# Branch results split into high and low parts where they are made, and eight modulation blocks placed behind branch b

## The chip, the cores and the metric

The kernel runs on one core of one Trainium2 chip. The metric is the device time of one execution in microseconds (us). Three executions before the change gave 1832.02, 1841.4 and 1842.75 us; their median, 1841.4, is the time before. One of them, the one that took 1842.75 us, was recorded by the hardware profiler, and all rows of the trace are from it.

## The reference

The kernel computes one layer of a streaming encoder for two request groups that share weights: one prompt of 1024 tokens and one sample of 64 tokens with a cache of 512 keys. All numbers are float32, the model is 1024 wide.

```
mod = silu(c) @ w_ada + b_ada
sh1, sc1, g1, sh2, sc2, g2 = split(mod, 6)

u = rmsnorm(x, norm1_g) * (1 + sc1) + sh1
sq, sk, sv, mqk, mv, mo, mi, mf, ga, gb = split(u @ w_in)
y_a = stick_breaking(sq, k_all, sv)          # 8 heads x 64
h   = mlstm(conv_silu(mqk), mv, mi, mf)      # 4 heads x 128
y_b = sigmoid(mo) * rmsnorm(h) * ml_norm_g

merged = sigmoid(ga) * (y_a @ w_a) + sigmoid(gb) * (y_b @ w_b)
x = x + g1 * (merged @ w_out)
u2 = rmsnorm(x, norm2_g) * (1 + sc2) + sh2
x = x + g2 * ((silu(u2 @ w_ff_gate) * (u2 @ w_ff_up)) @ w_ff_down)
y = rmsnorm(x, final_g)
```

Stick-breaking attention scores a key by a sigmoid and multiplies it by what the later keys have left over; on the chip this is a matmul for the scores, a scan on VectorE, transposes, and a matmul with the values. `y_a` and `y_b` are 512 columns each. `mod` has 6 x 1024 columns for each of the two groups, and they are computed in 48 blocks of 128 columns.

## The kernel before

**Data.** Activations lie transposed: 128 features on the partitions and all 1088 tokens (64 of the sample, then 1024 of the prompt) along the row. Work on tokens goes by three chunks, 0 to 320, 320 to 704 and 704 to 1088. A float32 product that needs its precision is made of three matmuls in the faster type fp32r (`mm3`, lines 75 to 78): both operands are split into a high part (rounded to fp32r) and a low part (the rest), and high x high, high x low and low x high are summed in PSUM. The helpers that split are `hi_act` (line 47, a copy on ScalarE), `hi_pool` and `lo_pool` (lines 53 and 59, GpSimd) and `lo_dve` (line 56, a subtraction on VectorE).

**Weights.** `w_unit` (lines 61 to 69) loads 512 KB of raw weights through the DMA queue of SyncE (SP) into a ring `wr` of three buffers and lets GpSimd (POOL) split it into the rings `wh` and `wl`. The 32 modulation blocks that are not needed at once load their 512 KB of `w_ada` into the same ring `wr` (tiles `wada`), 8 matmuls each in plain float32, a copy, a transpose and a sum (`ada_blocks`, lines 207 to 227).

**Stages.** Up to about 190 us the kernel normalises the input and computes the first modulation blocks. In the mLSTM stage (to about 500 us) the four mLSTM heads run beside the dense units of the input projection; at its end each head writes one 128 x 1088 tile `yb` to the DRAM scratch `yb_d` (lines 792 to 802). In the attention stage (to about 906 us) four pairs of heads run one after another. Pairs 0 to 2 run beside the units of the gates `ga` and `gb` and the modulation blocks 18 to 39, and each writes one tile `ya` to `ya_d` (line 559). Pair 3 runs beside what the change touches: `load_y` brings the seven tiles back as raw tiles `yr`, POOL splits them by chunk into `yh` and `yl` (seven tiles, three chunks, a high and a low part: 42 instructions), the last eight modulation blocks 40 to 47 follow, and then `branch_b`, which multiplies `y_b` by `w_b` in 24 pieces of 12 matmuls. A piece `ps_b` is copied by ScalarE into `tb`, multiplied by a loaded gate `lgb` on POOL and stored to `pb_d`; `lgb` and `tb` share a ring of four buffers, and `ps_b` has two PSUM banks. Pair 3's own `ya` is split on the spot. Branch a (lines 1025 to 1044, to about 961 us) multiplies `y_a` by `w_a` and adds the loaded `pb`: it needs two loads a piece (`lga`, `lpb`) and has six PSUM banks. `w_out` and the feed-forward follow.

**What sets the order.** The program does not write the engines' orders by hand. A call such as `run(attention(3), chain(fill), 27, 0)` advances an attention generator and a list of dense work beside each other; a scheduler with a timing model then places each instruction on its engine, in which the order of emission is the priority. On the chip each engine works its own list strictly in that order, and so does each DMA queue with the loads and stores given to it.

```
run(attention(3), chain(ada_left[24:32] + [branch_b()]), 27, 0)
```

The functions that the diff touches follow.

Of the kernel before, what the change touches and what calls it, by code (L numbers as in the profile page):

```python
# [8 lines left out]
F32 = mybir.dt.float32  # L9
F32R = mybir.dt.float32r  # L10
# [4 lines left out]
P = 128  # L15
# [20 lines left out]
def trunk(ctx, tc, a, o, dbg=None, stop=None):  # L36
# [9 lines left out]
    def hi_act(out, in_):  # L46
        nc.scalar.copy(out, in_)  # L47
# [4 lines left out]
    def hi_pool(out, in_):  # L52
        nc.gpsimd.tensor_scalar(out, in_, 1.0, 0.0, ALU.mult, ALU.add)  # L53

    def lo_dve(out, in_, h):
        nc.vector.tensor_sub(out, in_, h.bitcast(F32))  # L56

    def lo_pool(out, in_, h):
        nc.gpsimd.tensor_sub(out, in_, h.bitcast(F32))  # L59
# [80 lines left out]
    bif = const.tile([P, 8], F32, name="bif")  # L140


    ya_d = dram.tile([3, P, T], F32, name="ya_d")
    yb_d = dram.tile([4, P, T], F32, name="yb_d")
    ga_d = dram.tile([KB, P, T], F32, name="ga_d")
    gb_d = dram.tile([KB, P, T], F32, name="gb_d")
    pb_d = dram.tile([KB, P, T], F32, name="pb_d")
# [28 lines left out]
    def small(shape, name, tag, dtype=F32, bufs=2, pool=None):  # L176
        return (pool or cur["sb"]).tile(shape, dtype, tag=tag, name=name, bufs=bufs)

    def slot(shape, name, tag, bufs=1, dtype=F32):
        n = 1  # L180
        for d in shape[1:]:
            n *= d
        t = cur["sb"].tile([P, SIZES[tag]], dtype, tag=tag, name=name, bufs=bufs)
        v = t[: shape[0], :n]
        if len(shape) == 3:
            v = v.rearrange("p (x y) -> p x y", y=shape[2])
        return v
# [247 lines left out]
    def attention(p):  # L435
# [73 lines left out]
        for i in range(2):  # L509
            qs, kh, kl, vs = hd[i]  # L510
            for m in range(4):
# [34 lines left out]
                u0, u1 = (0, 64) if i == 0 else (64, 0)  # L546
                nc.scalar.copy(tmp[u0 : u0 + 64], po[u1 : u1 + 64, 0:256])
                nc.vector.tensor_add(ya[u0 : u0 + 64, qc], po[u0 : u0 + 64, 0:256], tmp[u0 : u0 + 64])
                if p == 3 and i == 1:
                    qc = slice(0 if m == 0 else NS + 256 * m, NS + 256 * (m + 1))  # L550
                    hi_act(yh[3][:, qc], ya[:, qc])
                    lo_dve(yl[3][:, qc], ya[:, qc], yh[3][:, qc])
                yield
            if i == 0:
                yield from sample()
                if p == 3:
                    y_tiles(3)
        if p < 3:
            nc.sync.dma_start(ya_d[p], ya)

# [152 lines left out]
    def mlstm(h):  # L715
# [73 lines left out]
        rsqrt_cols(cur["sb"], rd, mx, 9, "h")  # L789
        nc.vector.tensor_mul(hm, hm, rd[:, :, None].to_broadcast([P, 9, P]))  # L790
        yield
        yb = slot([P, T], f"yb{h}", "sg", 2)
        for c in range(3):
            ps = bank("t", f"ps_yb{h}_{c}", 3)
            s, e = CHUNKS[c]
            off = 0
            for tt in CTILES[c]:
                L = TILES[tt][1]
                nc.tensor.transpose(ps[:, off : off + L], hm[:L, tt, :], ident[:L, :L])
                off += L  # L800
            nc.vector.scalar_tensor_tensor(yb[:, s:e], ps[:, : e - s], mlg(h), st.og[:, s:e], ALU.mult, ALU.mult)
        nc.sync.dma_start(yb_d[h], yb)
        yield


# [31 lines left out]
    def chain(gens):  # L837
        for g in gens:
            yield from g
# [107 lines left out]
    def y_tiles(b):  # L947
        yh[b] = up.tile([P, T], F32R, tag="u", name=f"yh{b}")
        yl[b] = up.tile([P, T], F32R, tag="u", name=f"yl{b}")

    def load_y(bs):
        raw = {}
        for b in bs:
            raw[b] = up.tile([P, T], F32, tag="u", name=f"yr{b}")
            nc.sync.dma_start(raw[b], ya_d[b] if b < 4 else yb_d[b - 4])
            y_tiles(b)
        for s, e in CHUNKS:
            for b in bs:
                hi_pool(yh[b][:, s:e], raw[b][:, s:e])
                lo_pool(yl[b][:, s:e], raw[b][:, s:e], yh[b][:, s:e])  # L960

    def wide_unit(w, r0, nb, q, name):

# [28 lines left out]
            fill += gs[i : i + 1] + ads[i * na // ng : (i + 1) * na // ng]  # L992
        run(attention(p), chain(fill), 27, 0)
    wb0 = wide_unit(w_b, 0, 4, 0, "wb0")
    load_y(range(4, 8))
    for b in range(3):
        load_y([b])
    run(attention(3), chain(ada_left[24:32] + [branch_b()]), 27, 0)
    ph.close()


# [578 lines left out]
```

## Time and profile before

| | |
|---|---|
| time before, median of 3 (range) | 1841.4 us (1832.02 to 1842.75) |
| profiled execution's own time | 1842.75 us |
| its span in the trace | 1841.1 us |
| mean granted TensorE clock | 0.984 |
| TensorE (PE) busy | 1759.8 us, 96% of the span |
| VectorE (DVE) busy | 1006.8 us, 55% |
| GpSimd (POOL) busy | 677.5 us, 37% |
| ScalarE (ACT) busy | 671.0 us, 36% |

The span runs from the first to the last recorded instruction. Each row of the trace names a line of the kernel, an engine, an operation, the tiles it writes and reads (buffer numbers left out), shapes, a count and, in brackets, how long the engine stood idle before it and what ended the wait. A row of a timeline begins with the start time and the duration. A row for one tile (`yh<-yr x21: 448/512/2427`) gives the count, then shortest, median and longest duration in ns, then first and last start. `SPq` marks what SP issues to its DMA queue. The granted clock is the share of full speed that TensorE was allowed.

### The profile page before, as it was taken

The page shows a single profiled execution, that of the slowest core. Times are in us where ns is not written, and L with a number is a line of the kernel's source. Part 1 is how long each engine was busy: PE and PEld are TensorE (multiplying, and loading weights), DVE is VectorE, ACT ScalarE, POOL GpSimd, SP SyncE. Part 2 cuts the span into 40 slices and gives each one's busy share as a digit, 9 for nine tenths or more (in the row PEclk, how much of TensorE's full clock was granted, in tenths as well). Part 3 has the DMA queues.
Part 4 walks back from the last instruction along what each step waited for, and adds up shares of the span by engine and source line. Part 5 has one row for each costly group of instructions (what it writes and reads, how often), then busy time and mean ns, then how long its engine had stood idle before and what let it go on. Part 6 is the DMA issues. An engine that isn't in the chain of part 4 may idle for free. (4 is left out here: it accounts for less than half of the span.)

```text
span 1841.1 us, 31721 instructions
## 1 busy us (share of the span) xinstructions
PE 1759.8 (96%) x12388; PEld 1693.1 (92%) x12388; DVE 1006.8 (55%) x1903; ACT 671.0 (36%) x1401; POOL 677.5 (37%) x554
## 2 busy tenths in 40 slices
PE   5899999999999999988989999999999999999997
PEld 4699999999889888967979999999999999999997
DVE  6633424252267667785463488754555775544435
ACT  5332424343244444444313555532233543101006
POOL 2434645453433132387566330122222002354324
PEclk9999999999999999989999999999999999999999
DMA  9426667654756465694566246632222676443102
GB/s 268 112 81 198 164 189 154 196 126 137 173 149 145 122 150 134 157 264 133 174 192 186 72 140 196 180 92 79 71 77 77 207 203 197 159 144 114 47 12 98
DMA packets 313208, 265.54 MB, mean 144 GB/s; under 512 B 13670, under 2 KB 285282, under 8 KB 313058
## 3 DMA queue, kind: packets, MB, share of 16 engines
q1 hardware_dynamic: 301026, 224.67, 41.4%
q0 software_dynamic: 12032, 38.84, 9.2%
q8 instruction: 98, 1.61, 0.4%
q14 instruction: 52, 0.43, 0.1%
HBM read 206.62 MB, written 77.84 MB: 155 GB/s over the span
## 5 line engine op out<-in xcount | busy, mean ns | idle before, releaser
L76 PE MATMUL ps_fd<-hh,wh_fd 128*128 128x384 f32 (+1 forms) x480 | 157.1, 327 | 1.2 <-DVE hst L1348 1.2
L78 PE MATMUL ps_fd<-hh,wl_fd 128*128 128x384 f32 (+1 forms) x480 | 157.2, 327 | 0.0
L77 PE MATMUL ps_fd<-hl,wh_fd 128*128 128x384 f32 (+1 forms) x480 | 157.1, 327 | 0.0
L56 DVE TENSOR_TENSOR w<-wr,w 128x512 fp32r<-128x512 f32 x140 | 95.6, 694 | 38.5 <-ACT w L47 35.5
L1432 DVE SCALAR_TENSOR_TENSOR x1f<-ps_fd,mod,x1f 128x384 f32<-128x384 f32 (+2 forms) x128 | 60.4, 497 | 101.3 <-PE ps_fd L78 101.3
L390 DVE TENSOR_TENSOR_SCAN re<-re 128x128 f32<-128x128 f32 (+3 forms) x64 | 105.5, 1651 | 15.7 <-ACT re L386 15.4
L47 ACT CAST w<-wr 128x512 fp32r<-128x512 f32 x140 | 85.2, 620 | 74.7 <-PE ps_gc L1356 21.1
L53 POOL TENSOR_SCALAR wh_fd<-wr_fd 128x1024 fp32r<-128x1024 f32 x20 | 24.6, 1232 | 227.1 <-PE ps_ga L1356 119.4
L76 PEld LDWEIGHTS ps_fd<-hh,wh_fd 128*128 128x128 f32 x480 | 90.1, 188 | 1.4 <-POOL wl_fd L59 1.4
L78 PEld LDWEIGHTS ps_fd<-hh,wl_fd 128*128 128x128 f32 x480 | 90.1, 188 | 0.0
L77 PEld LDWEIGHTS ps_fd<-hl,wh_fd 128*128 128x128 f32 x480 | 90.1, 188 | 0.0
L47 ACT CAST hh<-hr 128x1088 fp32r<-128x1088 f32 (+1 forms) x26 | 24.1, 962 | 175.5 <-PE ps_fd L77 151.4
L386 ACT ACTIVATE re<-z 128x512 f32<-128x512 f32 (+2 forms) x96 | 47.3, 494 | 81.5 <-DVE z L382 67.5
L1356 PE MATMUL ps_ga<-b1h,w 128*128 128x272 f32 x352 | 74.3, 290 | 2.5 <-ACT g L1341 1.8
L1356 PE MATMUL ps_gb<-b6h,w 128*128 128x272 f32 x352 | 75.2, 292 | 0.0
L1356 PE MATMUL ps_gd<-b7h,w 128*128 128x272 f32 x352 | 75.0, 292 | 0.0
L1356 PE MATMUL ps_ga<-b2h,w 128*128 128x272 f32 x352 | 74.1, 289 | 0.0
L1356 PE MATMUL ps_gc<-b5h,w 128*128 128x272 f32 x352 | 74.1, 290 | 0.0
L1356 PE MATMUL ps_gc<-b3h,w 128*128 128x272 f32 x352 | 73.7, 288 | 0.0
L1356 PE MATMUL ps_gd<-b4h,w 128*128 128x272 f32 x352 | 73.6, 289 | 0.0
L56 DVE TENSOR_TENSOR al<-ps_a,ah 128x512 fp32r<-128x512 f32 (+1 forms) x80 | 49.4, 630 | 34.2 <-ACT ah L47 33.8
L76 PE MATMUL ps_ga<-uh,wh_ga 128*128 128x384 f32 (+1 forms) x192 | 64.9, 338 | 1.5 <-DVE re L388 1.2
(551 smaller groups left out, 6067.4 us busy)
## 6 DMA issues: line engine op xcount, KB each, us to landing
wada<-in_w_ada SPq DMA_DIRECT2D x48, 512.0 KB
wr<-wsum_d SPq DMA_DIRECT2D x80, 256.0 KB
h_d<-hst SPq DMA_DIRECT2D x44, 272.0 KB
wr<-in_w_ff_gate SPq DMA_DIRECT2D x40, 256.0 KB
wr_fd<-in_w_ff_down SPq DMA_DIRECT2D x20, 512.0 KB
hr<-h_d SPq DMA_DIRECT2D x18, 544.0 KB
wsum_d<-in_w_ff_up POOLq DMA_DIRECT2D x6, 1282.0 KB, 7.8
wsum_d<-in_w_ff_gate POOLq DMA_DIRECT2D x6, 1282.0 KB, 7.8
```

The costliest lines, as they stand in the source:

```text
L47: nc.scalar.copy(out, in_)
L53: nc.gpsimd.tensor_scalar(out, in_, 1.0, 0.0, ALU.mult, ALU.add)
L56: nc.vector.tensor_sub(out, in_, h.bitcast(F32))
L76: nc.tensor.matmul(ps, wh, xh, start=first, stop=False)
L77: nc.tensor.matmul(ps, wh, xl, start=False, stop=False)
L78: nc.tensor.matmul(ps, wl, xh, start=False, stop=last)
L386: nc.scalar.activation(rest[:, c0 : c0 + w], ps, AF.Sigmoid, scale=-scale)
L390: nc.vector.tensor_tensor_scan(r, r, r, 1.0, ALU.mult, ALU.bypass)
L1356: nc.tensor.matmul(ps, w[:, a, j, :], b[j // 2][:, j % 2, :], start=p in (1, 6, 5, 7) and j == 0 and k == 0, stop=j == 3 and k == 2, skip_ ...
L1432: nc.vector.scalar_tensor_tensor(x1[m][:, lo:hi], ps[:, lo - s : hi - s], mod[:, 40 + m, g : g + 1], x1[m][:, lo:hi], ALU.mult, ALU.add)
```

## The change

The two scratch arrays get a second plane, so that each branch result is kept as its high and its low part.

- An mLSTM head (`yb`) no longer collects one tile: for each chunk it makes the piece, splits it with ScalarE and VectorE, and stores both parts. 4 heads x 3 chunks give 12 casts, 12 subtractions and 24 stores, in place of 4 stores.
- An attention pair 0 to 2 splits `ya` in four pieces as they are finished (the first of 320 tokens, with the sample), through two small tiles with one buffer each, and stores both parts: again 12 casts, 12 subtractions and 24 stores, in place of 3.
- `load_y` loads the parts straight into `yh` and `yl`: 14 loads of 544 KB in place of 7, and the 42 instructions on POOL and the raw tiles are gone.
- Beside pair 3, branch b is emitted first and the modulation blocks 40 to 47 behind it.

What is computed and every matmul on it stay the same.

```diff
--- before.py
+++ after.py
@@ -140,8 +140,8 @@
     bif = const.tile([P, 8], F32, name="bif")
 
 
-    ya_d = dram.tile([3, P, T], F32, name="ya_d")
-    yb_d = dram.tile([4, P, T], F32, name="yb_d")
+    ya_d = dram.tile([3, 2, P, T], F32, name="ya_d")
+    yb_d = dram.tile([4, 2, P, T], F32, name="yb_d")
     ga_d = dram.tile([KB, P, T], F32, name="ga_d")
     gb_d = dram.tile([KB, P, T], F32, name="gb_d")
     pb_d = dram.tile([KB, P, T], F32, name="pb_d")
@@ -546,17 +546,22 @@
                 u0, u1 = (0, 64) if i == 0 else (64, 0)
                 nc.scalar.copy(tmp[u0 : u0 + 64], po[u1 : u1 + 64, 0:256])
                 nc.vector.tensor_add(ya[u0 : u0 + 64, qc], po[u0 : u0 + 64, 0:256], tmp[u0 : u0 + 64])
-                if p == 3 and i == 1:
+                if i == 1:
                     qc = slice(0 if m == 0 else NS + 256 * m, NS + 256 * (m + 1))
-                    hi_act(yh[3][:, qc], ya[:, qc])
-                    lo_dve(yl[3][:, qc], ya[:, qc], yh[3][:, qc])
+                    if p == 3:
+                        h_, l_ = yh[3][:, qc], yl[3][:, qc]
+                    else:
+                        h_, l_ = (small([P, 320], f"yp{x}{p}_{m}", f"yp{x}", F32R, bufs=1)[:, : qc.stop - qc.start] for x in "hl")
+                    hi_act(h_, ya[:, qc])
+                    lo_dve(l_, ya[:, qc], h_)
+                    if p < 3:
+                        nc.sync.dma_start(ya_d[p, 0, :, qc], h_.bitcast(F32))
+                        nc.sync.dma_start(ya_d[p, 1, :, qc], l_.bitcast(F32))
                 yield
             if i == 0:
                 yield from sample()
                 if p == 3:
                     y_tiles(3)
-        if p < 3:
-            nc.sync.dma_start(ya_d[p], ya)
 
 
 
@@ -789,7 +794,6 @@
         rsqrt_cols(cur["sb"], rd, mx, 9, "h")
         nc.vector.tensor_mul(hm, hm, rd[:, :, None].to_broadcast([P, 9, P]))
         yield
-        yb = slot([P, T], f"yb{h}", "sg", 2)
         for c in range(3):
             ps = bank("t", f"ps_yb{h}_{c}", 3)
             s, e = CHUNKS[c]
@@ -798,8 +802,15 @@
                 L = TILES[tt][1]
                 nc.tensor.transpose(ps[:, off : off + L], hm[:L, tt, :], ident[:L, :L])
                 off += L
-            nc.vector.scalar_tensor_tensor(yb[:, s:e], ps[:, : e - s], mlg(h), st.og[:, s:e], ALU.mult, ALU.mult)
-        nc.sync.dma_start(yb_d[h], yb)
+            n = e - s
+            yb = small([P, 384], f"yb{h}_{c}", "gt")[:, :n]
+            h_ = small([P, 384], f"ybh{h}_{c}", "sh", F32R)[:, :n]
+            l_ = small([P, 384], f"ybl{h}_{c}", "sl", F32R)[:, :n]
+            nc.vector.scalar_tensor_tensor(yb, ps[:, :n], mlg(h), st.og[:, s:e], ALU.mult, ALU.mult)
+            hi_act(h_, yb)
+            lo_dve(l_, yb, h_)
+            nc.sync.dma_start(yb_d[h, 0, :, s:e], h_.bitcast(F32))
+            nc.sync.dma_start(yb_d[h, 1, :, s:e], l_.bitcast(F32))
         yield
 
 
@@ -948,16 +959,11 @@
         yh[b] = up.tile([P, T], F32R, tag="u", name=f"yh{b}")
         yl[b] = up.tile([P, T], F32R, tag="u", name=f"yl{b}")
 
-    def load_y(bs):
-        raw = {}
-        for b in bs:
-            raw[b] = up.tile([P, T], F32, tag="u", name=f"yr{b}")
-            nc.sync.dma_start(raw[b], ya_d[b] if b < 4 else yb_d[b - 4])
-            y_tiles(b)
-        for s, e in CHUNKS:
-            for b in bs:
-                hi_pool(yh[b][:, s:e], raw[b][:, s:e])
-                lo_pool(yl[b][:, s:e], raw[b][:, s:e], yh[b][:, s:e])
+    def load_y(b):
+        y_tiles(b)
+        src = ya_d[b] if b < 4 else yb_d[b - 4]
+        for t, x in ((yh[b], 0), (yl[b], 1)):
+            nc.sync.dma_start(t.bitcast(F32), src[x])
 
     def wide_unit(w, r0, nb, q, name):
 
@@ -992,10 +998,9 @@
             fill += gs[i : i + 1] + ads[i * na // ng : (i + 1) * na // ng]
         run(attention(p), chain(fill), 27, 0)
     wb0 = wide_unit(w_b, 0, 4, 0, "wb0")
-    load_y(range(4, 8))
-    for b in range(3):
-        load_y([b])
-    run(attention(3), chain(ada_left[24:32] + [branch_b()]), 27, 0)
+    for b in (4, 5, 6, 7, 0, 1, 2):
+        load_y(b)
+    run(attention(3), chain([branch_b()] + ada_left[24:32]), 27, 0)
     ph.close()
 
 
```

The scheduler's order moves with it. First, PE where branch b begins. In the rows `po2_1_3` is the output of attention pair 2, `z3` are scores of pair 3, `ps_ada40` is modulation block 40, `ps_b0_0` the first piece of branch b with the parts `yh4` to `yh7` of `y_b` and the weights `wh_wb0`, `wl_wb0`. Before:

```order
L541 MATMUL po2_1_3_7724<-ah_2_1_3_4_7756,vs2_1_7188 128x256
L217 MATMUL ps_ada40_8967<-wada40_8968,cT_85 32x128 x8
L520 MATMUL z3_0_4_0_8471<-kh3_0_8353,qs3_0_8352 128x512
L521 MATMUL z3_0_4_0_8471<-kl3_0_8354,qs3_0_8352 128x512
L541 MATMUL po2_1_3_7724<-al_2_1_3_4_7757,vs2_1_7188 128x256
L541 MATMUL po2_1_3_7724<-ah_2_1_3_4_7756,vs2_1_7188 128x256
L541 MATMUL po2_1_3_7724<-al_2_1_3_4_7757,vs2_1_7188 128x256
```

After:

```order
L541 MATMUL po2_1_3_7864<-ah_2_1_3_4_7896,vs2_1_7310 128x256
L76 MATMUL ps_b0_0_9070<-yh4_8427,wh_wb0_8423 128x320
L77 MATMUL ps_b0_0_9070<-yl4_8428,wh_wb0_8423 128x320
L78 MATMUL ps_b0_0_9070<-yh4_8427,wl_wb0_8424 128x320
L76 MATMUL ps_b0_0_9070<-yh5_8431,wh_wb0_8423 128x320
L77 MATMUL ps_b0_0_9070<-yl5_8432,wh_wb0_8423 128x320
L78 MATMUL ps_b0_0_9070<-yh5_8431,wl_wb0_8424 128x320
L76 MATMUL ps_b0_0_9070<-yh6_8435,wh_wb0_8423 128x320
L541 MATMUL po2_1_3_7864<-al_2_1_3_4_7897,vs2_1_7310 128x256
L541 MATMUL po2_1_3_7864<-ah_2_1_3_4_7896,vs2_1_7310 128x256
L541 MATMUL po2_1_3_7864<-al_2_1_3_4_7897,vs2_1_7310 128x256
```

Where block 40 stood between two matmuls of pair 2's last output, the first seven matmuls of branch b stand, and its next ones are spread among attention's from there.

Second, PE at the end of branch b; `ps_b7_2` is its last piece and `ps_a0_0` the first of branch a. Before:

```order
L77 MATMUL ps_b7_2_9550<-yl7_8297,wh_wb6_9451 128x384
L78 MATMUL ps_b7_2_9550<-yh7_8296,wl_wb6_9452 128x384
L76 MATMUL ps_a0_0_9625<-yh0_8324,wh_wa0_9617 128x320
L77 MATMUL ps_a0_0_9625<-yl0_8325,wh_wa0_9617 128x320
L78 MATMUL ps_a0_0_9625<-yh0_8324,wl_wa0_9618 128x320
```

After:

```order
L78 MATMUL ps_b7_2_9525<-yh7_8439,wl_wb6_9427 128x384
L217 MATMUL ps_ada40_9544<-wada40_9545,cT_85 32x128 x8
L541 MATMUL po3_1_3_9013<-ah_3_1_3_4_9045,vs3_1_8469 128x256
L217 MATMUL ps_ada41_9560<-wada41_9561,cT_85 32x128 x5
L541 MATMUL po3_1_3_9013<-al_3_1_3_4_9046,vs3_1_8469 128x256
L541 MATMUL po3_1_3_9013<-ah_3_1_3_4_9045,vs3_1_8469 128x256
```

and some rows on:

```order
L217 MATMUL ps_ada46_9640<-wada46_9641,cT_85 32x128 x8
L222 MATMUL ps_ada46_9640<-ident_66,ada_sb46_9651 128x128
L217 MATMUL ps_ada47_9656<-wada47_9657,cT_85 32x128 x8
L222 MATMUL ps_ada47_9656<-ident_66,ada_sb47_9667 128x128
L76 MATMUL ps_a0_0_9728<-yh0_8443,wh_wa0_9720 128x320
L77 MATMUL ps_a0_0_9728<-yl0_8444,wh_wa0_9720 128x320
```

The eight blocks and the last matmuls of attention now stand between the two branches.

Third, SP's queue at the same place. `pb_d<-tb7_1` and `tb7_2` are the stores of branch b's last pieces, `wada` the raw weights of a modulation block, `wr_wa` those of branch a, `lga` and `lpb` the loads for branch a's first pieces. Before:

```order
L983 DMA pb_d_98<-tb7_1_9546 128x384
L983 DMA pb_d_98<-tb7_2_9565 128x384
L1033 DMA lga0_0_9621<-ga_d_96 128x320
L1033 DMA lpb0_0_9623<-pb_d_98 128x320
L1033 DMA lga0_1_9642<-ga_d_96 128x384
L1033 DMA lpb0_1_9644<-pb_d_98 128x384
```

After:

```order
L989 DMA pb_d_98<-tb7_1_9521 128x384
L214 DMA wada43_9593<-in_w_ada 128x8x128
L989 DMA pb_d_98<-tb7_2_9540 128x384
L214 DMA wada44_9609<-in_w_ada 128x8x128
L214 DMA wada45_9625<-in_w_ada 128x8x128
L214 DMA wada46_9641<-in_w_ada 128x8x128
L214 DMA wada47_9657<-in_w_ada 128x8x128
L64 DMA wr_wa0_9718<-in_w_a 128x4x256
L64 DMA wr_wa2_9854<-in_w_a 128x4x256
L64 DMA wr_wa4_9990<-in_w_a 128x4x256
L1038 DMA lga0_0_9724<-ga_d_96 128x320
```

The loads of blocks 43 to 47 and of branch a's first three weights, which stood far ahead of these stores, now stand around and behind them, and ahead of branch a's first gate loads.

## The prediction

> **What bounds the kernel now.** The page comes first.
>
> ```profile
> span 1841.1 us, 31721 instructions
> PE 1759.8 (96%) x12388; PEld 1693.1 (92%) x12388; DVE 1006.8 (55%) x1903; ACT 671.0 (36%) x1401; POOL 677.5 (37%) x554
> ```
>
> TensorE (PE) is busy for 1759.8 of 1841.1 us, so a change gains only by taking away PE idle time (81 us in all), slow clock or PE work. The table by stage shows where these lie; its columns are the stretch, its length, the busy time of PE, PEld, DVE, ACT and POOL with instruction counts, the granted PE clock, the DMA share and GB/s.
>
> ```profile
> 190.00:500.00 310.00, 305.87 (x1968) 298.66 (x1967) 109.59 (x225) 112.24 (x241) 145.07 (x129) 1.00 0.63 161
> 500.00:787.00 287.00, 274.00 (x1920) 249.52 (x1920) 201.52 (x378) 126.55 (x296) 87.59 (x88) 0.98 0.60 146
> 787.00:826.00 39.00, 32.04 (x289) 23.39 (x291) 36.01 (x79) 18.94 (x43) 34.33 (x32) 0.87 0.92 270
> 826.00:839.00 13.00, 11.22 (x86) 10.84 (x78) 5.16 (x14) 5.21 (x13) 13.00 (x15) 1.00 0.33 116
> 839.00:852.00 13.00, 8.94 (x31) 7.47 (x32) 6.02 (x11) 3.60 (x9) 7.77 (x9) 0.74 0.40 127
> 852.00:906.00 54.00, 50.86 (x326) 48.51 (x325) 32.03 (x46) 24.34 (x58) 34.74 (x24) 1.00 0.49 152
> 906.00:961.00 55.00, 49.52 (x293) 47.67 (x291) 30.63 (x43) 10.69 (x27) 35.52 (x29) 1.00 0.66 195
> ```
>
> The stretch that the change rewrites is 787 to 906, between the last gate unit and branch a. In its first 39 us VectorE (DVE) is busy for 36.0 and POOL for 34.3, while PE idles for 7.0 and runs at 0.87 of its clock: attention's scans set the pace and PE has nothing dense beside them. PE's order in time shows why.
>
> ```profile
> 799.08 0.39 PE L541 MATMUL po<-al,vs 128*128 128x256 f32 x1 [1.69 <-DVE al L56]
> 815.12 0.33 PE L222 MATMUL ps_ada<-ident,ada_sb 128*128 128x128 f32 x1 [2.47 <-DVE ada_sb L220]
> 826.26 0.41 PE L76 MATMUL ps_b<-yh,wh_wb 128*128 128x320 f32 x1
> 840.49 0.50 PE L474 MATMUL z0s<-ckl,zq 128*128 128x512 f32 x1 [3.26 <-POOL ckl L53]
> 906.29 0.33 PE L78 MATMUL ps_b<-yh,wl_wb 128*128 128x384 f32 x1
> 906.47 0.31 PE L76 MATMUL ps_a<-yh,wh_wa 128*128 128x320 f32 x1
> ```
>
> Branch b, the dense work of this stretch, begins at 826.3 and ends at 906.6; branch a follows without a gap. What held branch b back is seen in the instructions on the raw tiles `yr`.
>
> ```profile
> L53 POOL TENSOR_SCALAR yh<-yr x21: 448/512/2427, 791.6 to 835.1; 128x384 fp32r<-128x384 f32 x14, 128x320 fp32r<-128x320 f32 x7
> L59 POOL TENSOR_TENSOR yl<-yr,yh x21: 857/1000/2498, 793.1 to 841.5; 128x384 fp32r<-128x384 f32 x14, 128x320 fp32r<-128x320 f32 x7
> L955 SPq DMA_DIRECT2D yr<-yb_d x4: 338/392/479, 782.5 to 785.6; - x4
>   DMA yr<-yb_d: 7.6, 1
> ```
>
> Loads go out from 782.5, POOL waits until 791.6 and then splits 42 pieces until past 841.
>
> **The change, part by part.** Times are the profiled execution's: span 1841.1, its own time 1842.75, 1.3 over the median 1841.4 and the highest of the three runs.
>
> POOL issues the loads of an attention head beside those of `yr`.
>
> ```profile
> 780.83 1.12 POOL L430 DMA_DIRECT2D kh<-qk_d  x2 [2.81 <-PE z L521]
> 781.92 0.54 POOL L429 DMA_DIRECT2D qs<-qk_d  x1
> 782.42 0.55 POOL L431 DMA_DIRECT2D kl<-qk_d  x1
> 782.92 0.57 POOL L429 DMA_DIRECT2D qs<-qk_d  x1
> 783.42 0.58 POOL L431 DMA_DIRECT2D kl<-qk_d  x1
> ```
>
> *The split leaves POOL.* All 42 POOL operations go. Two prices rise from it. Eight tiles of 544 KB instead of four must land before branch b's first chunk can end: 4.46 MB at the 270 GB/s of 787 to 826 are 16.5 us, so from 782.5 the last lands near 799. That head's six loads of 64 rows (272 KB each) share the wires: 1.67 MB or 6 us more, so 805 is the late end. I take 803. And the freed POOL no longer slows VectorE:
>
> ```profile
> 755.31 0.42 DVE L391 TENSOR_TENSOR be<-be,re 128x256 f32<-128x256 f32 x1
> 794.75 0.91 DVE L391 TENSOR_TENSOR be<-be,re 128x256 f32<-128x256 f32 x1
> ```
>
> The same product takes 0.42 us beside a quiet POOL and 0.91 beside the splits. A few such pairs make 2 to 4 us of VectorE time in a stretch that VectorE bounds.
>
> *Eight modulation blocks leave the front.* One block is 16 matmul records and a transpose (the row groups two blocks):
>
> ```profile
> 810.15 1.08 PE L217 MATMUL ps_ada<-wada,cT 128*32 128x128 f32 x32 [0.17 <-DVE mod L227]
> ```
>
> Half of 1.08 us and about 0.2 for the transpose make 0.75 each, 6 us for eight.
>
> *What this gives up to the end of branch b.* The ceiling: idle time 7.0 + 1.8 + 4.1 + 3.1 = 16.0 (table), clock 32.04 x 0.13 + 8.94 x 0.26 = 6.5, blocks 6: 28.5 us. What comes back: until 803 PE has attention alone, as before (16 us at the 18% idle of that stretch are 3 us), and it is in-order, with branch b's first matmuls standing ahead of attention's, so a tile that lands late stops both: 4 more (0 to 9). The 87 us after it keep the 6% idle of 852 to 906, 5 us, plus 2 for `ckl`, whose 3.26 us wait was for a POOL that is now free. Clock 1.5. So 28.5 - 15.5 = **13 us earlier**, between 5 and 20: branch b ends near 893.
>
> *What the blocks cost behind branch b.* Blocks 43 to 47 need buffers of the three-deep `wr` ring that blocks 40 to 45 hold, and the weights of branch a come behind them in the same ring and on the same SP queue. So once branch b ends there is a chain of loads with nothing dense on PE. How long a 512 KB load takes from issue to its waiting reader is seen twice:
>
> ```profile
> 578.27 0.38 SPq L64 DMA_DIRECT2D wr_gb<-in_w_in  x1
> 582.53 1.04 POOL L53 TENSOR_SCALAR wh_gb<-wr_gb 128x1024 fp32r<-128x1024 f32 x1 [11.36 <-DMA wr_gb<-in_w_in]
> 651.87 0.38 SPq L64 DMA_DIRECT2D wr_gb<-in_w_in  x1
> 661.67 1.04 POOL L53 TENSOR_SCALAR wh_gb<-wr_gb 128x1024 fp32r<-128x1024 f32 x1 [8.87 <-DMA wr_gb<-in_w_in]
> ```
>
> 4.3 us at best, 9.8 at worst. And the end of branch b on POOL, with the splits of branch a's weights:
>
> ```profile
> 907.11 1.01 POOL L982 TENSOR_TENSOR tb<-tb,lgb 128x384 f32<-128x384 f32 x1 [2.37 <-DMA lgb<-gb_d]
> 909.56 1.01 POOL L982 TENSOR_TENSOR tb<-tb,lgb 128x384 f32<-128x384 f32 x1 [0.42 <-DMA lgb<-gb_d]
> 910.53 2.40 POOL L59 TENSOR_TENSOR wl_wa<-wr_wa,wh_wa 128x1024 fp32r<-128x1024 f32 x1
> 914.39 0.87 POOL L1039 TENSOR_TENSOR lga<-lga,lpb 128x320 f32<-128x320 f32 x1 [1.46 <-DMA lpb<-pb_d]
> ```
>
> The last two products end 1.5 and 4.0 us after the last matmul of branch b (906.6), and SP's order puts the load of block 43 behind the store of the one, 44 and 45 behind the other. From branch b's end: load 43 goes out at 2.0, 44 and 45 at 4.5 and 4.9. They land at 6.3, 8.8 and 10.7 (512 KB at 270 GB/s is 1.9 us, so the third waits for the wire). Block 45 computes by 11.3, its buffer takes the first weights of branch a, which land at 15.6; POOL's high part (1.04) opens branch a at 16.7, with 12 matmuls that need no low part (2 us), and the low part is there 2.4 us later, at 19. PE meanwhile has 6 us of blocks. Branch a starts in effect **17 us after branch b's end**, where it was 0: 14 if the loads overlap better, 26 at 9.8 us a load.
>
> The Trainium skill ("DMA: Bandwidth & Descriptors", section "Anatomy of one DMA — SWDGE (gpsimd) path") fits a DMA as 2.0 us plus bytes over 436 GB/s, 3.2 us for 512 KB. By it the two loads in series would be 2 us shorter and the gap an estimated 15 us. The 4.3 us of the row is the time here, so it stands.
>
> *After a gap PE's clock is low:* 839 to 852 ran at 0.74, 13 x 0.26 = 3.4 us lost. I take 2.5 (0 to 4). *Branch a's own queue:* POOL holds three splits (3.4 us each) ahead of the first `lga` sum, which so comes some 10 us after branch a's start instead of 8: 2 us (0 to 4), hidden by six PSUM banks at first.
>
> *Where the splits went.* 24 casts on ScalarE (ACT) and 24 subtractions on VectorE:
>
> ```profile
> L47 ACT CAST yh<-ya 128x256 fp32r<-128x256 f32 (+1 forms) x4 | 1.7, 428 | 2.0 <-DVE ya L548 2.0
> L56 DVE TENSOR_TENSOR yl<-ya,yh 128x256 fp32r<-128x256 f32 (+1 forms) x4 | 3.0, 744 | 0.5 <-ACT yh L47 0.5
> ```
>
> 10 us on the one, 18 on the other. Before 500, half of each lies under PE at 305.87 of 310; without that cover it would be 14 us. The `sh` ring is now shared with the q and k results, so a cast waits for a store two back: 0 to 1 us for each head. In 500 to 787 VectorE is busy for 201 of 287, and 6 us more there delay attention a little. SP also gets 41 more stores, of which some wait ahead of weight loads with a ring's slack. Together +2 (-2 to 6).
>
> **The sum:** -13 + 17 + 2.5 + 2 + 2 = +10.5 on 1842.75, or 1853; two of the terms (clock, `lga`) may overlap with each other, so I take **1851**. The parts' ends give 1834 to 1868.
>
> **The rivals.** Bounds first: about 1% (18 us: under 1823, over 1860) is what a measurement tells from no change.
>
> 1. *Slow chain, slower.* The place is the loads between block 43 and branch a's first weights. Near 9 us a load and above, the gap is 26 us and the time 1860. For it: 651.87 to 661.67, and eight 512 KB loads with branch a's first `lga` and `lpb` share that stretch. Against: the quick row, and no attention loads are left by then. 20%.
> 2. *Branch b is no earlier.* It waits for twice the bytes, or SP, held by the store of pair 2's last low part (it stands ahead of `lgb1_0`), starves the four `gt` buffers. Then only the 6 us of blocks are gained: 1858, with a third of its chance above 1860. 13%.
> 3. *The gap is filled.* Attention's tail runs late and covers the chain, or VectorE's relief brings the full 20 us: 1830 to 1840. 11%.
> 4. *No gap at all and the full gain:* 1842.75 - 20 is 1823 and below. Against it stands the ring: a block's buffer frees only after PE has read it. 6%.
>
> The forecast itself has 50%. Slower by over 1%: 26% (rival 1, part of 2, 2% of the forecast); faster by over 1%: 7%; within: 67%. The range that holds 8 in 10 is **1834 to 1867**.
>
> **What will show it.** Right: no `yr` on POOL; the first `ps_b` near 796 to 804 and the last near 893; `ps_ada` in a row behind it with PE mostly idle for 12 to 20 us; POOL's first `wh_wa` ended by a DMA, and `ps_a` from about 910. Wrong: a first `ps_b` after 815 (rival 2), a gap under 8 us (rivals 3, 4) or above 24 (rival 1), or PE idle time before 787 that grew by more than 5 us.

## The result, and the profile after

The changed kernel takes 1860.7 us in the median of five executions against 1841.6 in the median of six before, measured beside it: a ratio of 1.0106 (95% interval 1.009 to 1.0123), about 19 us slower. A sixth execution (4505.21 us), and one of the run ya_split_only below (7697.19 us), fell in a slow state of the chip and are left out. The profiled execution took 1856.07 us, 13.3 more than the profiled one of before. The rows below account for these 13.3; the rest is scatter between executions, since the profiled one of before was the slowest of its series and that of after one of the fastest of its own.

The table by stage starts at 190 us in both kernels and is then cut at the same events: from 190 us to the last transpose of the mLSTM result (`ps_yb`), to the last gate unit (`ps_gb`), to the last matmul of branch b, (after the change) to the first of branch a, to the first of `w_out`, to the end. Columns are the stretch, its length, busy time of PE, PEld, DVE, ACT and POOL, granted PE clock, DMA share, GB/s. Before:

```profile
190.00:482.80 292.80, 292.34 (x1888) 286.10 (x1887) 107.51 (x218) 110.48 (x238) 135.91 (x115) 1.00 0.60 158
482.80:787.50 304.70, 288.02 (x2003) 262.36 (x2001) 203.98 (x386) 128.31 (x300) 96.75 (x102) 0.98 0.63 151
787.50:906.60 119.10, 103.16 (x722) 90.53 (x722) 78.86 (x147) 52.42 (x122) 89.84 (x77) 0.93 0.60 184
906.60:961.70 55.10, 49.62 (x296) 47.70 (x294) 31.33 (x45) 10.43 (x26) 35.79 (x30) 1.00 0.67 195
961.70:1841.10 879.40, 861.34 (x6297) 856.81 (x6294) 494.50 (x906) 297.98 (x573) 247.16 (x167) 0.99 0.41 124
```

After:

```profile
190.00:497.00 307.00, 294.44 (x1875) 287.79 (x1873) 123.43 (x224) 108.96 (x240) 135.29 (x114) 0.98 0.58 153
497.00:802.20 305.20, 282.16 (x2003) 261.32 (x2001) 205.80 (x398) 135.43 (x316) 96.24 (x100) 0.97 0.62 158
802.20:904.60 102.40, 91.27 (x577) 83.38 (x576) 71.44 (x122) 51.38 (x121) 43.24 (x35) 0.93 0.68 211
904.60:921.60 17.00, 11.35 (x145) 6.57 (x144) 7.32 (x29) 1.79 (x5) 2.06 (x2) 0.70 0.89 252
921.60:974.90 53.30, 50.89 (x294) 49.61 (x295) 30.06 (x43) 9.49 (x24) 38.55 (x29) 0.97 0.70 211
974.90:1854.30 879.40, 860.73 (x6294) 855.98 (x6294) 493.54 (x906) 298.62 (x574) 247.57 (x168) 0.99 0.41 124
```

By stage, after minus before: mLSTM +14.2, attention beside the gates +0.5, branch b -16.7, gap +17.0, branch a -1.8, the rest 0.0: together +13.2. Branch b's gain and the gap cancel; what is left is the mLSTM stage, where PE had idled 0.46 us and now idles 12.56 (the other 2.1 us are busy time, at a clock of 0.98 for 1.00). The waits of PE (what waits for what, us in total, times, longest) show on whom. Before the change the largest wait of `ps_yb` was 0.5 us; after it, between 190 and 560:

```profile
PE ps_ga L76 <- ACT gt_ga L823: 15.1, 1, 15.1
PE ps_yb L803 <- DVE hn L795: 11.8, 3, 4.8
```

The second row is the loss of the mLSTM stage: PE stands at the transposes of three heads because VectorE's normalised result `hn` is late. (The first row lies at the start of attention. That stage as a whole is only 0.5 us longer, but ya_split_only below, without the split of `yb`, is 6.1 us shorter there.) Why `hn` is late is seen in the first head. Before, VectorE:

```profile
208.42 1.79 DVE L735 TENSOR_SCALAR wg<-W 128x8 f32<-128x8 f32 x1 [1.32 <-ACT W L733]
212.63 0.22 DVE L84 RECIPROCAL rd<-rs_h 128x9 f32<-128x9 f32 x1 [0.87 <-ACT rs_h L83]
212.88 1.18 DVE L85 TENSOR_TENSOR rs_h<-rd 128x9 f32<-128x9 f32 x1
214.71 1.36 DVE L790 TENSOR_TENSOR hn<-hn,rd 128x1152 f32<-128x1152 f32 x1
```

After, VectorE, then ScalarE, then POOL:

```profile
207.04 4.33 DVE L740 TENSOR_SCALAR wg<-W 128x8 f32<-128x8 f32 x1 [1.32 <-ACT W L738]
215.33 0.22 DVE L84 RECIPROCAL rd<-rs_h 128x9 f32<-128x9 f32 x1 [2.50 <-ACT rs_h L83]
215.58 3.86 DVE L85 TENSOR_TENSOR rs_h<-rd 128x9 f32<-128x9 f32 x1
220.10 1.36 DVE L795 TENSOR_TENSOR hn<-hn,rd 128x1152 f32<-128x1152 f32 x1
...
212.66 1.12 ACT L704 ACTIVATE cs<-cv 128x1091 f32<-128x1091 f32 x1 [3.47 <-DVE mx L792]
213.80 1.28 ACT L83 ACT_TABLE_LOAD   x1
215.09 0.21 ACT L83 ACTIVATE rs_h<-mx 128x9 f32<-128x9 f32 x1
...
207.42 2.91 POOL L705 TENSOR_TENSOR cv<-cv,cs 128x1091 f32<-128x1091 f32 x1
209.95 1.39 POOL L53 TENSOR_SCALAR wh_v<-wr_v 128x1024 fp32r<-128x1024 f32 x1
214.19 2.93 POOL L705 TENSOR_TENSOR cv<-cv,cs 128x1091 f32<-128x1091 f32 x1
216.70 2.71 POOL L59 TENSOR_TENSOR wl_v<-wr_v,wh_v 128x1024 fp32r<-128x1024 f32 x1
```

The work between is the convolution of the next head: `cs` on ScalarE and the product `cv` on POOL. Before, it came behind the normalisation (the two products began at 221.28 and 225.05); now it runs through its middle. ScalarE does `cs` ahead of `rs_h` (VectorE's wait is 2.50 for 0.87): the square root `rs_h` stands behind 1.12 us of `cs` and behind the row ACT_TABLE_LOAD of 1.28 us, which before the change began at 211.09, while `mx` was still being made. And two VectorE operations on 8 or 9 elements a row last 4.33 and 3.86 us, for 1.79 and 1.18, beside POOL's products. The reason is in one removed line of the diff: `yb` had held a slot of the ring `sg`, which has two, and `cs` needs one. With `yb` in small tiles the slot is free, and the scheduler moves the next head's convolution ahead (raw_gt below tests this). The third user of `sg` is `hsq`, the squares of the normalisation itself. The wait of 3.47 us in the first row of ScalarE ends with the sum over them (`mx`, L792), which fits a second `cs` that now takes the slot of `hsq`.

The gap behind branch b, SP's loads first, then PE and POOL:

```profile
905.32 0.38 SPq L214 DMA_DIRECT2D wada<-in_w_ada  x1
915.70 4.35 SPq L64 DMA_DIRECT2D wr_wa<-in_w_a  x3
...
912.64 1.08 PE L217 MATMUL ps_ada<-wada,cT 128*32 128x128 f32 x16 [1.48 <-DMA wada<-in_w_ada]
914.57 1.08 PE L217 MATMUL ps_ada<-wada,cT 128*32 128x128 f32 x16
921.63 0.64 PE L76 MATMUL ps_a<-yh,wh_wa 128*128 128x320 f32 x1 [1.12 <-POOL wh_wa L53]
...
920.53 1.05 POOL L53 TENSOR_SCALAR wh_wa<-wr_wa 128x1024 fp32r<-128x1024 f32 x1 [13.82 <-PE ps_ada L222]
```

The matmul at 912.64 is block 44. Its load went out at 907.36, the first of four in one more row of SP:

```profile
907.36 6.77 SPq L214 DMA_DIRECT2D wada<-in_w_ada  x4
```

So the gap is a chain: 2.7 us until block 41 has freed a buffer, 5.3 for the load of block 44, 3.1 for blocks 44 and 45 (45 begins 1.9 us after 44, behind its copy and transpose; the gap's clock is 0.70), whose second frees the buffer at 915.70, 4.8 for branch a's first weights, 1.1 for their split: 17.0.

### The profile page after: what moved, and what is told of

The parts are those of the page before. It is cut to its first block, busy times and chain, and to the rows that moved or that the text cites. A ratio compares the mean times of both kernels' runs of the same rounds, so it can differ in the third digit from the quotient of the medians.

```text
span 1854.3 us, 31842 instructions
## 1 busy us (share of the span) xinstructions
PE 1758.3 (95%) x12388; PEld 1695.5 (91%) x12388; DVE 1024.3 (55%) x1927; ACT 677.3 (37%) x1423; POOL 634.6 (34%) x512
## 5 line engine op out<-in xcount | busy, mean ns | idle before, releaser
L390 DVE TENSOR_TENSOR_SCAN re<-re 128x128 f32<-128x128 f32 (+3 forms) x64 | 94.5, 1478 | 13.9 <-ACT re L386 13.3
L76 PE MATMUL ps_ga<-uh,wh_ga 128*128 128x384 f32 (+1 forms) x192 | 65.0, 338 | 15.1 <-ACT gt_ga L823 15.1
```

What stands on the lines that cost most here:

```text
L76: nc.tensor.matmul(ps, wh, xh, start=first, stop=False)
L390: nc.vector.tensor_tensor_scan(r, r, r, 1.0, ALU.mult, ALU.bypass)
```

## The experiments

Each run stands beside executions of the kernel before on the same chip. The third column is the time from the first to the last `ps_yb`, which lies in the mLSTM stage alone, as in these rows of the tile before and after the change (218.5 to 482.8 is 264.3). What the first head loses ahead of its `ps_yb` is not in it: that row began at 214.2 to 218.5 us in the runs in which `yb` has its slot, and at 220.2 to 224.1 in those in which it has none. In the table, the fourth column is the gap from branch b's last matmul to branch a's first.

```profile
L799 PE MATMUL ps_yb<-ident,hn x36: 271/273/332, 218.5 to 482.8; 128*128 128x128 f32 x32, 64*128 64x64 f32 x4
```

```profile
L803 PE MATMUL ps_yb<-ident,hn x36: 271/327/473, 221.5 to 497.0; 128*128 128x128 f32 x32, 64*128 64x64 f32 x4
```

| run | ratio to before (95%) | mLSTM heads, us | gap, us |
|---|---|---|---|
| before | 1 | 264.3 | 0.2 |
| the change | 1.0106 (1.009 to 1.0123) | 275.5 | 17.0 |
| order_only | 1.0061 (1.0042 to 1.0081) | 264.3 | 16.7 |
| split_only | 1.0049 (1.0031 to 1.0067) | 277.0 | 0.2 |
| ya_alone | 0.9955 (0.9941 to 0.997) | 264.3 | 0.2 |
| yb_alone | 1.012 (1.0102 to 1.0138) | 275.5 | 3.6 |
| ya_split_only (ya and order) | 0.9991 (0.9974 to 1.0007) | 264.3 | 17.5 |
| yb_in_slot | 1.0046 (1.0028 to 1.0065) | 278.7 | 18.7 |
| slot_mix | 1.0002 (0.999 to 1.0013) | 279.3 | 0.2 |
| inplace_mix | 1.0032 (1.0017 to 1.0047) | 280.4 | 0.2 |
| dead_casts | 0.9987 (0.9975 to 0.9999) | 264.3 | 16.4 |
| raw_gt | 1.0144 (1.0115 to 1.0172) | 277.5 | 16.3 |
| gt3 | 1.0113 (1.0087 to 1.0139) | 275.7 | 18.9 |
| ya_mix | 0.9962 (0.9945 to 0.9979) | 264.2 | 0.2 |
| ya_pieces | 0.9972 (0.9958 to 0.9986) | 264.3 | 0.2 |
| tail3 | 0.9928 (0.9906 to 0.9951) | 264.2 | 6.4 |

**The order alone** (order_only), on the kernel before:

```diff
-    run(attention(3), chain(ada_left[24:32] + [branch_b()]), 27, 0)
+    run(attention(3), chain([branch_b()] + ada_left[24:32]), 27, 0)
```

> The kernel before with only the emission order changed: branch b ahead of blocks 40 to 47, splits on GpSimd as before. Theory 1 (the chain is the order's own cost): a gap of 13 to 20 us between the last matmul of branch b and the first of branch a; the mLSTM stage is unchanged (last ps_yb near 483); branch b gains at most the 6 us of the blocks, so 1848 to 1858, slower than before by 6 to 16. Rival (without the early end the tail of attention covers the loads): 1838 to 1845 and no gap over 8 us.

1.0061 (1852.0 us), as theory 1 had it. The gap is there in full, on an untouched mLSTM stage, so it belongs to the order:

```profile
786.10:898.00 111.90, 94.14 (x577) 85.85 (x576) 76.21 (x121) 51.03 (x119) 73.15 (x74) 0.92 0.52 155
898.00:914.70 16.70, 10.93 (x145) 6.05 (x144) 6.33 (x27) 1.84 (x5) 2.06 (x2) 0.78 0.92 261
```

Branch b's stretch falls by 7.2 us (119.1 before). Its first matmul stands at 800.4 instead of 826.3 although POOL still splits 42 pieces: the blocks ahead of it had held its start, not the splits alone.

**The splits alone** (split_only): the changed kernel with that line as before.

> The changed kernel with blocks 40 to 47 emitted ahead of branch b again. Theory 1 (load chain behind branch b costs 17 us, the blocks in front cost 6 and delay branch b some): branch a follows branch b without a gap over 3 us, the time is 1846 to 1853, 6 to 14 below the changed kernel; the mLSTM stage stays as slow as in the changed kernel. Rival (VectorE's scans or the twice as large loads bound the stretch, and the gap only took up slack that branch b's early end had made): the time stays at 1855 to 1863.

1.0049, the forecast of theory 1: no gap, and the mLSTM stage as slow as in the change.

**`ya` without `yb`** (ya_split_only): the changed kernel with `yb` of before, as one tile in its slot, stored raw and split by POOL at branch b.

> The changed kernel with yb as before (one tile a head, stored raw, loaded raw and split on GpSimd), so that only ya is split where it is made; branch b still ahead of blocks 40 to 47. Theory 1 (the mLSTM stage's loss comes only from the split of yb: slot, rings and stores): from 190 us to the last ps_yb 293 us as before (307 in the changed kernel), gap ahead of branch a 17 us. For the attention stage two outcomes: if the split of ya shortens it (it freed the ya tile earlier), the last ps_gb falls 292 to 299 us behind the last ps_yb (304.8 before) and the time is 1840 to 1846; if not, 303 to 307 and 1847 to 1856, like the kernel with the order alone. Theory 2 (mLSTM stage slow for another reason): last ps_yb at 492 or later.

The ratio is 0.9991 (1836.5 us), better than expected for either outcome, with 299.1 us from the last `ps_yb` to the last `ps_gb`, at the edge of the first. The heads take 264.3 us as before, and the new order with `ya` split costs nothing in sum. So the split of `yb` is worth 1.0106 - 0.9991 = 1.15%, 21 us, all of the change's loss. Between the two profiles it makes the mLSTM stage 14.6 us longer and the stretch from there to the last gate unit 6.1 (305.2 against 299.1), and branch b 5.1 shorter. With `ya` raw and the order alone that stretch was 305.8, so beside the new order the split of `ya` gains there about what the split of `yb` loses. This does not add up as simply in the old order: in yb_alone below, with `ya` raw, it is 298.1.

**Each split alone** (ya_alone, yb_alone), in the order of before.

> The kernel before with the split of ya alone (parts stored per piece, loaded straight into yh and yl); yb raw and split on GpSimd, blocks 40 to 47 ahead of branch b as before. If the parts add up (ya split beside the new order: 0.9991 against 1.0061, so -0.70%), the ratio to before is 0.991 to 0.995, 1822 to 1830 us. Rival (the split of ya only helps the early branch b of the new order): 0.998 to 1.002, 1835 to 1842.

> The kernel before with the split of yb alone (as in the change: no slot, parts in the rings gt, sh and sl); ya raw, order as before. If the parts add up (the change 1.0106 against 0.9991 without the split of yb, so +1.15%), the ratio is 1.010 to 1.014, with the last ps_yb near 497. Rival (what yb's split costs ahead of 500 is regained in the attention stage when nothing else is changed, as the wait on gt_ga was): 0.999 to 1.005.

The split of `yb` costs what the sum of the parts said, 1.2%. That of `ya` gains 0.45%, where 0.7% was expected; the intervals of the three ratios are too wide to tell the two apart.

**What of `yb`'s split costs.** First its slot back (yb_in_slot), the lines that differ from the change:

```diff
+        yb_all = slot([P, T], f"yb{h}", "sg", 2)
-            yb = small([P, 384], f"yb{h}_{c}", "gt")[:, :n]
+            yb = yb_all[:, s:e]
```

> The changed kernel, but yb of an mLSTM head is again collected in a slot of the two-deep ring sg and split from there. Theory 1 (freed slot): in the changed kernel the conv work of the next head (cs on ScalarE, its product on GpSimd) no longer waits for yb's slot, runs ahead of the head's normalisation and delays hn; with yb back in the ring the conv falls behind again, the last ps_yb starts near 483 to 488 us (497 in the changed kernel, 483 before) and the time is 1842 to 1850 us, 10 to 16 below the changed kernel. Theory 2 (the 24 casts, 24 subtractions and 24 stores themselves, in rings shared with q and k, are the load): nothing of this is removed, the last ps_yb stays at 494 or later and the time at 1855 to 1863.

The total followed theory 1 (1.0046), but only half of its reason held: the waits on `hn` were gone (0.5 us), yet the heads took 278.7 us and the last `ps_yb` stood at 496.4, as theory 2 had it. The waits of PE show a new one:

```profile
PE ps_k L76 <- DVE sl L56: 11.1, 2, 5.8
```

and the timeline shows where it begins, at the end of the first head, on ScalarE and then on PE:

```profile
227.15 0.51 ACT L47 CAST ybh<-yb 128x384 fp32r<-128x384 f32 x1 [7.17 <-DMA yb_d<-ybh]
...
229.07 0.60 PE L76 MATMUL ps_k<-uh,wh_k 128*128 128x320 f32 x1 [5.30 <-DVE sl L56]
```

The third cast of a head finds both buffers of `sh` held by stores under way and waits 7.17 us for the first to land. ScalarE and VectorE, which work in order, stand with it; the results of the q unit stay in PSUM; PE stops at the k unit. In the profile the total's gain over the change lies around this stage: the first `ps_yb` is 3.8 us earlier, and the stretch from the last `ps_yb` to the last gate unit, with 6.7 us of waits on `gt_ga` for 15.1, is 7.2 shorter.

To get round these rings, the parts were laid into two slots of `sg`, the low part over `yb`, with the blocks spread as in slot_mix below (inplace_mix):

> As slot_mix, but the parts of yb lie in two slots of the ring sg (the low part over yb itself) in place of the two-deep rings sh and sl that q and k use. Theory 1 (in slot_mix the third cast of a head waited 7 us for the store of the first, and q's and k's evacuation stood behind it): no PE wait on sl above 1 us in the mLSTM stage, which takes 293 to 296 us from 190 us (303.5 from 190 in slot_mix), time 1826 to 1833. Rival (the casts and subtractions themselves fill ScalarE and VectorE, or the next head's conv now waits for two stores): the stage stays above 300 us and the time at 1837 to 1842.

A miss: 1.0032, and the heads no faster. No wait on `sl` is left, but two others are in its place:

```profile
PE ps_yb L805 <- DVE hn L795: 7.6, 1, 7.6
...
PE ps_S L749 <- POOL cv L705: 5.0, 2, 2.7
```

The second fits a convolution that now needs both slots back and comes too late for the next head's scores; the first was not followed up. Three forms had been slow with different waits, so the parts of the edit were tried one by one. The casts and subtractions alone, their results stored nowhere and never read (dead_casts; its main lines, as against ya_split_only):

```diff
+            h_ = small([P, 384], f"ybh{h}_{c}", "sh", F32R)[:, :n]
+            l_ = small([P, 384], f"ybl{h}_{c}", "sl", F32R)[:, :n]
+            hi_act(h_, yb[:, s:e])
+            lo_dve(l_, yb[:, s:e], h_)
```

> As ya_split_only (yb stored raw from its slot), with the 12 casts and 12 subtractions of yb still made into the rings sh and sl, but their results stored nowhere and read by nobody. Theory 1 (it is the landing of the part stores, for which the next cast in a two-deep ring waits, that costs in yb_in_slot): the mLSTM stage takes 291 to 296 us from 190 us, no PE wait on sl above 1.5 us, ratio 0.998 to 1.002. Theory 2 (the casts and subtractions themselves, ahead of q's and k's evacuation on ScalarE and VectorE, cost): 300 us or more, ratio 1.004 to 1.008.

And the freed slot without casts (raw_gt), again the main lines as against ya_split_only. `yb` has to lie somewhere, so its pieces take the ring `gt`, as in the change, and are stored from there:

```diff
-        yb = slot([P, T], f"yb{h}", "sg", 2)
+            yb = small([P, 384], f"yb{h}_{c}", "gt")[:, : e - s]
+            nc.sync.dma_start(yb_d[h][:, s:e], yb)
-        nc.sync.dma_start(yb_d[h], yb)
```

> As ya_split_only, but yb is made in the ring gt by chunk, as in the change, and stored raw by chunk: no casts, no parts, and the ring sg has a slot more for the next head's conv. Theory 1 (the freed slot alone brings the changed kernel's waits on hn, with the conv ahead of the normalisation in ScalarE's order): PE waits 8 us or more on hn, the mLSTM stage takes 302 to 308 us, ratio 1.006 to 1.012. Theory 2 (the splits and their stores bring them): the stage takes 291 to 297 us, ratio 0.998 to 1.002.

The two are as far apart as they could be. With all casts and subtractions the stage runs at full PE load; with none, but the slot freed, it has the changed kernel's waits. The stage with the dead casts first, then that with the freed slot, and the latter's wait:

```profile
190.00:479.50 289.50, 289.04 (x1868) 282.74 (x1867) 109.43 (x221) 114.19 (x246) 136.65 (x115) 1.00 0.60 158
```

```profile
190.00:497.70 307.70, 295.17 (x1864) 288.67 (x1863) 117.67 (x212) 104.09 (x231) 135.15 (x114) 0.97 0.57 148
```

```profile
PE ps_yb L803 <- DVE hn L795: 12.5, 3, 5.3
```

The first head of raw_gt has the delays of the changed kernel, on VectorE:

```profile
205.55 4.32 DVE L740 TENSOR_SCALAR wg<-W 128x8 f32<-128x8 f32 x1 [1.32 <-ACT W L738]
213.82 0.21 DVE L84 RECIPROCAL rd<-rs_h 128x9 f32<-128x9 f32 x1 [2.50 <-ACT rs_h L83]
214.07 4.02 DVE L85 TENSOR_TENSOR rs_h<-rd 128x9 f32<-128x9 f32 x1
```

In dead_casts the same three figures are 1.80, 0.86 and 1.19. The first piece of `yb` is written at 221.13, behind these rows, so neither the ring `gt` nor a store of `yb` can have caused them; the free slot is what is left.

That settles the mLSTM stage: the 24 operations that the forecast had priced cost nothing, and the slot that it had not looked at costs the stage. The landing of stores in a shared ring is a second price, shown by yb_in_slot. The ratio of raw_gt, 1.0144, is above what either theory had. Against ya_split_only its profile has 15.3 us more in the mLSTM stage and 14.7 more from there to the last gate unit (313.8 against 299.1), with a wait of 17.9 on `gt_ga`. This second part fits the ring `gt`, in which VectorE waits 15.5 us in all for stores of `yb` to land; it was not tested apart from the slot.

**The wait on `gt_ga`** (gt3): the changed kernel with three buffers instead of two in the ring `gt` of the mLSTM stage.

> The changed kernel with a gt ring of three buffers in place of two in the mLSTM stage. Theory 1 (the 13 us that PE waits more at the start of attention are lost on the spot and regained before the last ps_gb, so the wait costs nothing): the wait on gt_ga falls below 9 us (15.1), but the time from the last ps_yb to the last ps_gb stays at 302 to 308 us, the time at 1855 to 1863. Rival (the wait is on the path): that stretch falls to 290 to 298 and the time to 1843 to 1852.

The ratio stays, 1.0113, while the wait is halved and the stretch to the last gate unit is 6.4 us shorter (298.8 for 305.2), which neither theory had:

```profile
PE ps_ga L76 <- ACT gt_ga L823: 7.6, 1, 7.6
```

```profile
499.80:798.60 298.80, 282.87 (x2003) 262.41 (x2000) 205.05 (x398) 135.22 (x316) 98.26 (x100) 0.97 0.63 162
```

In the profile the mLSTM stage is 2.8 us longer (190 to 499.8), branch b with the gap 1.9 and the last stage 3.6. So the wait is not worth its 15 us at the end; why the 6.4 were given back stays open.

**The gap.** Spreading the blocks through branch b, first with `yb` in its slot (slot_mix), then with `yb` raw (ya_mix):

```diff
-    run(attention(3), chain([branch_b()] + ada_left[24:32]), 27, 0)
+    def mixed():
+        ads = ada_left[24:32]
+        for n_, _ in enumerate(branch_b()):
+            yield
+            if n_ % 3 == 1:
+                yield from ads[n_ // 3]
+    run(attention(3), mixed(), 27, 0)
```

> yb back in its slot as in yb_in_slot, and one modulation block after every third piece of branch b, in place of eight behind it. Theory 1 (both losses are separate from the gain of branch b's part, 16.7 us): the mLSTM stage as before, no gap ahead of branch a over 4 us, time 1824 to 1836. Rival (the blocks' loads share the three-deep wr ring with branch b's weights, so the wait moves into branch b): 1838 to 1848, with PE idle waits on POOL wh_wb inside branch b.

> As ya_split_only, with one modulation block after every third piece of branch b instead of eight behind it. Theory 1: no gap, no loss in the mLSTM stage, time 1826 to 1837, faster than before. Rival (GpSimd's splits of yb hold branch b back again once the blocks are beside it): the stretch from the last ps_gb to the last ps_b is 116 us or more and the time 1838 to 1846.

Neither has a gap. Against the same kernels with the blocks behind, slot_mix gains 0.44% and ya_mix 0.29%. The first missed its forecast, with the mLSTM stage as slow as in yb_in_slot; the second is faster than before, as expected. Then only as many blocks behind branch b as `wr` has buffers (tail3, on ya_split_only):

```diff
-    run(attention(3), chain([branch_b()] + ada_left[24:32]), 27, 0)
+    run(attention(3), chain(ada_left[24:29] + [branch_b()] + ada_left[29:32]), 27, 0)
```

> As ya_split_only, but only blocks 45 to 47 behind branch b, five ahead of it. The three behind fit the three buffers of wr, so their loads can be there before branch b ends. Theory 1 (the gap is a chain of two loads in series, a block's and then branch a's weights): one load is left, the gap between the last ps_b and the first ps_a is 6 to 11 us (17.6 in ya_split_only), ratio 0.993 to 0.997. Rival (the gap is PE's own serial work on the blocks and the store of branch b's last pieces): the gap is 13 us or more, ratio 0.997 to 1.001.

The gap is 6.4 us and holds one load, of branch a's weights, from 885.86 to 890.18:

```profile
885.86 0.94 SPq L64 DMA_DIRECT2D wr_wa<-in_w_a  x2
...
890.18 1.05 POOL L53 TENSOR_SCALAR wh_wa<-wr_wa 128x1024 fp32r<-128x1024 f32 x1 [3.61 <-DMA wr_wa<-in_w_a]
```

At 0.9928 it has the lowest ratio of the study, 13 us under the kernel before: `ya` split, `yb` raw, five blocks ahead of branch b and three behind.

**Why `ya`'s split gains** (ya_pieces): the kernel before with `ya` stored raw in four pieces and nothing else.

> The kernel before with ya stored raw in four pieces as they are finished, and nothing else: the splits of ya and yb stay on GpSimd. Theory 1 (the split of ya gains because GpSimd has 18 operations less beside the last pair): no gain here, ratio 0.998 to 1.002. Theory 2 (it gains because the tile ya, of which there is one, comes free for the next pair without waiting for one store of 544 KB): ratio 0.992 to 0.996.

0.9972 lies between the two theories, and its interval overlaps with that of ya_alone, so storing by pieces may give part of the gain or all of it. In its profile, though, the stretch from the last `ps_yb` to the last gate unit, where pairs 0 to 2 would gain by theory 2, is no shorter than before (306.2 us against 304.7; 300.4 in ya_alone). Why the split of `ya` gains stays open.

## Why the prediction was right and wrong

The direction was right and the measured time lies in the range, but the size was off: 9.6 us slower was forecast (1851 against 1841.4), about 19 measured. By its steps:

- **Branch b ends 13 us earlier.** Its stretch from the last gate unit shrank by 16.7, within the 5 to 20. The first `ps_b` came 12.2 us after the last gate unit, at 799.7 if the 14.7 us lost ahead of it are taken off; 796 to 804 was forecast. Part of the mechanism was another: by order_only the order alone gives 7 of it. VectorE was relieved, though not in the product that the forecast had named (L391: 1.05 us in the mean in this stretch before, 1.08 after), but in the 16 scans of pair 3, which took 3.0 us less. Before (787.5 to 906.6), then after (802.2 to 904.6):

```profile
L390 DVE TENSOR_TENSOR_SCAN re<-re 128x128 f32<-128x128 f32 (+7 forms) x16 | 27.0, 1688 | 6.0 <-ACT re L386 6.0
```

```profile
L390 DVE TENSOR_TENSOR_SCAN re<-re 128x128 f32<-128x128 f32 (+7 forms) x16 | 24.0, 1502 | 4.0 <-ACT re L386 3.9
```

- **The gap of 17 us.** It measured 17.0, and 16.3 to 18.9 wherever all eight blocks stood behind branch b. Its chain of two loads is the one that was forecast: block 45 was done 11.1 us after branch b's end (11.3 forecast) and branch a's first weights were there after 15.9 (15.6). The loads took 5.3 and 4.8 us, where the row gave 4.3; the Trainium skill's formula in "DMA: Bandwidth & Descriptors", section "Anatomy of one DMA — SWDGE (gpsimd) path", gives 3.2. It is fitted to transfers that GpSimd issues; SP issued these, and the formula is too low for them here.
- **Clock and branch a's queue, 4.5 us.** Not seen in sum: branch a's stretch was 1.8 us shorter. Its clock was 0.97 for 1.00 and PE was busy for 1.3 us more, but PE idled 3.1 less. The low clock, 0.70, lay inside the gap, whose 17 us include it.
- **The sum for the attention side** was so +8.5, and measured -1.5.
- **"Where the splits went", +2 (-2 to 6).** This is the step that failed: the stages ahead of branch b measured +14.7 in the profile, after what `ya`'s split gains there, and `yb`'s split cost 21 us by the ratios. It counted casts, subtractions and stores, and found them covered by PE at 305.87 of 310 us. dead_casts shows that this was right for the casts. Not counted was the slot of `sg` that the removed tile gave back, and with it the conv that moved into the normalisation. The ring `sh`, put at 0 to 1 us a head, made casts wait for stores 4.6 us in all in the change and 17.0 in yb_in_slot, 7.17 of them in the first head.
- **The rivals.** None came to pass: branch b was earlier, the gap had its forecast size, and no rival lay ahead of 787 us. Only the last sign named there, PE idle time before 787 that grows by more than 5 us, was the right one: between 190 us and the last gate unit it grew from 17.1 to 35.6.

So two errors of opposite sign, -10 on the attention side and +13 ahead of it, left a sum that was closer than its parts. That the time fell into the range was luck to this extent.

## What to carry to other kernels

A tile that an edit removes is also a place in a ring: list who else uses that ring, since the next user will start earlier, and ask what it will run beside; here that made the mLSTM stage 15.3 us longer (raw_gt against ya_split_only), while everything the edit computes there cost nothing (dead_casts). Results that go to DRAM through a two-deep ring made the third one wait for a landing (7.17 us in yb_in_slot), and with it all that stood behind it on its engine. And work moved behind a stage needs its inputs loaded by then: three blocks, as many as there are buffers, left a gap of 6.4 us with one load, and eight left one of 17 with a chain of two.

## What the runs showed of the hardware

A VectorE operation on 9 elements a row lasted 3.86 us beside POOL in the first head of the changed kernel, and 4.12 in the second, where its like took 1.18 and 1.15 before. The product at L85 began at 215.58 and ended at 219.44, 0.03 us after POOL's `wl_v` (216.70 + 2.71), which had followed `cv` without a pause; the scaling at L740 ended at 211.37, 0.03 after `wh_v`. Before the change L85 ended at 214.06, just behind `wl_v` too:

```profile
211.61 2.42 POOL L59 TENSOR_TENSOR wl_v<-wr_v,wh_v 128x1024 fp32r<-128x1024 f32 x1
```

The Trainium skill ("SBUF — State Buffer", section "Who interferes with whom") says that a VectorE instruction with two inputs in SBUF contends with a GpSimd instruction that reads SBUF, for a port pair that is locked for a whole instruction. The rows of L85, whose two inputs lie in SBUF, agree; this operation, begun during `cv`, did not end before `wl_v` did, so it seems to have got no turn between two POOL instructions that followed each other directly. L740 has one input tile, so that sentence does not cover it, and it lasted just as long; why is not shown.
